# Another program order in the RWKV mixers: the merges of a head pair move behind the projections of the next pair

## The chip, the cores and the metric

The kernel runs on one core of a Trainium2 chip. The metric is the device time of one execution in microseconds. Three runs of the kernel before stand on record.

## The reference, cut to what matters

A first block of two layers (each a token mixer with RWKV and convolution branches, then a mixture of experts, "PEER") is followed by a second block with other mixers. The change lies in the RWKV branch of the two token mixers.

```python
def rwkv_scan(decay, k, v, kk, a, r, s0, reverse):
...
    def step(S, inp):
        w_t, k_t, v_t, kk_t, a_t = inp[:5]
        sa = jnp.einsum('bhvk,bhk->bhv', S, kk_t)
        S = (S * w_t[:, :, None, :]
             - sa[..., None] * (kk_t * a_t)[:, :, None, :]
             + v_t[..., None] * k_t[:, :, None, :])
        y = jnp.einsum('bhvk,bhk->bhv', S, inp[5]) if emit else None
        return S, y
...
def rwkv_branch(zr, p, s0, emit):
...
    for d, (w1d, a1d) in enumerate(((w1f, a1f), (w1b, a1b))):
        wlog = -jax.nn.softplus(-(p['w0'][d] + jnp.tanh(w1d) @ p['w2'][d])) - 0.5
        decay = jnp.exp(-jnp.exp(wlog.astype(jnp.float32)))
        a = jax.nn.sigmoid(a1d @ p['a2'][d] + p['a0'][d])
        kd = k * (1 + (a - 1) * p['k_a'])
        S, y = rwkv_scan(heads(decay), heads(kd), heads(v), kk, heads(a),
                         heads(r) if emit else None, s0[d], reverse=(d == 1))
```

There are 16 heads of 64 channels, a forward and a backward scan, and 512 tokens (256 of context, 256 of the sequence). Layer 0 needs the outputs of all tokens, layer 1 those of the sequence alone.

## The kernel before, in words

The scan is computed in chunks of 64 tokens. Two heads (a pair, j = 0 to 7) fill the 128 partitions. For each pair `rwkv_a` projects k, r and v (the tiles `zps`, 72 matmuls, each product in three parts of high and low halves, all issued by the helper at L264), norms k (`ssps`, L425), makes decay and gate (`wps` and `aps`, L442, each followed by a tanh on ScalarE, L445), and then the chunks' score matrices (`scps`, L491), transposes (`btps`, L505; `vps`, L515) and the bonus (`bops`, L524).

`rwkv_inv` inverts the triangular score matrices: `tri_inverse` in layer 0, `tri_inverse16` in layer 1. Each has two halves. The head takes blocks to DRAM and back, runs a forward substitution row by row on VectorE (`tm`, `xt`: 31 steps in layer 0, 15 in layer 1) and sends the result through DRAM into `xl`. The tail, here called the merges, joins the inverted blocks by 32x32 matmuls into `q` (L686 and L692 in layer 0: 128 of them; L750, L759, L772 and L780 in layer 1: 384 of them) with copies on ScalarE and VectorE between the groups.

`rwkv_b` is the serial chain over the 8 chunks in both directions: `bp`, a copy to `bs`, `up`, a copy to `uv`, `zp`, a scaling into `zb`, and the outputs `yp`; then mean and variance (`mps`, L619; `vaps`, L624). The loop runs chain j-1 after `rwkv_a(j)` and the inversion of pair j.

Independent work fills the gaps: convolution tiles (C), gate projections (G, the tiles `gtps`, 24 matmuls each), modulation weights (A, `adaps`), the gate of the RWKV output (I, also `zps`), layer norm sums (M, V), the convolution's output product (B, `yb`). The table `PLAN` says at which named places (`pop("a")`, `pop("z")`, `pop("i")`, `pop("c0")` and so on) one of each kind is issued. A scheduler turns the program into one queue per engine: the program order sets the priority, and a ready instruction may pass one that is not ready. Psum tiles come from shared pools of two buffers each: "mm" for all projections and fills, "rk" for `ssps` through `q`.

Of the kernel before, what the change touches and what calls it, by code (L numbers as in the profile page):

```python
# [27 lines left out]
NPAIR = 8  # L28
# [4 lines left out]
PLAN = (({'s1': 'C', 'a': 'GGAA', 'i': 'AC'}, {'c4': 'GGA', 'c5': 'A', 'c7': 'AC'}, {'z': 'GAMIGI', 'i': 'V', 'c0': 'S', 'c1': 'S'}, {'c0': 'OA', 'c1': 'O', 'c2': 'O', 'c3': 'B', 'c4': 'A'}),  # L33
        ({'z': 'G', 's0': 'AC', 's1': 'GCAAG', 'i': 'G'}, {'z': 'G', 'c0': 'G', 'c1': 'AA', 'c2': 'C'}, {'z': 'I', 'i': 'I', 'c0': 'MVS', 'c7': 'S'}, {}))
BUMP = (200, 400)
W16 = (0, 1, 1)
# [142 lines left out]
class Core:  # L179
# [225 lines left out]

    def rwkv_a(self, l, j, emitc):

        nc, rp, pr = self.nc, self.rp, self.prk
        Tr = T2 if emitc else TX
        emit = lambda c: emitc or c < 4  # L410
# [22 lines left out]
        SC, KR, BT, UV, kds = [], [], [], [], []  # L433
        pcs = rp.tile([P, 2, 8], F32, tag="pcs", name="pcs", bufs=2)
# [3 lines left out]
        for q, (src, bias, res, name) in enumerate(((self.tw, self.w0h, lds, "ld"), (self.za, self.a0h, ths, "th"))):  # L438
# [4 lines left out]
            for d in range(2):  # L443
                t = tl(name)
                nc.scalar.activation(t, pss[d], AF.Tanh, scale=0.5, bias=bias[:, d, j:j + 1])  # L445
                res.append(t)
        self.pop("z")
        for d in range(2):
            ld, th = lds[d], ths[d]

# [68 lines left out]
        bo = tl("bo", "bo", 2)  # L519
# [4 lines left out]
        nc.tensor.matmul(ps[:, :Tr], self.blk, bo[:, :Tr], start=True, stop=True)  # L524
        nc.vector.tensor_mul(bo[:, :Tr], v[:, :Tr], ps[:, :Tr])
        nc.scalar.activation(bo[:, :Tr], bo[:, :Tr], AF.Identity, bias=self.par(l, "lnx_b", j))
        return SC, KR, BT, UV, pcs, bo

    def rwkv_inv(self, l, ops):
        (self.tri_inverse, self.tri_inverse16)[W16[l]]([[t[:, 0].rearrange("p c h t -> p (c h) t") for t in q]  # L530
                                                        for q in ops[0]], self.prk, ("rk", "rk"))

    def rwkv_b(self, l, j, emitc, o, ops):

# [101 lines left out]
    def tri_inverse(self, SC, pp, tag):  # L636


        nc, rp = self.nc, self.rp
        ND = len(SC)  # L640
        NL = 32 * ND
        s0 = self.dp.tile([2, 2, 16, 32, 32], F32, tag="inv0", name="inv0")
        s1 = self.dp.tile([2, 2, 16, 16, 2, 32], F32, tag="inv1", name="inv1")
        xd = rp.tile([64, 16, 32], F32, tag="i2", name="xd", bufs=4)
        halves = [(t, slice(8 * n, 8 * n + 8)) for n, t in enumerate(SC[0])]
        for b in range(2):
            bs = slice(32 * b, 32 * b + 32)
            for n, (t, us) in enumerate(halves):
                nc.vector.transpose(xd[bs, us], t[bs, :, bs])
                if ND > 1:  # L650
                    nc.sync.dma_start(s0[1, b, us].rearrange("u s t -> s u t"), SC[1][n][bs, :, bs])
            nc.sync.dma_start(s0[0, b].rearrange("u s t -> s u t"), xd[bs])

        am = rp.tile([2 * NL, 32, 32], F32, tag="am", name="am", bufs=1)
        xt = rp.tile([2 * NL, 16, 32], F32, tag="xt", name="xt", bufs=1)
        nc.gpsimd.memset(xt, 0.0)
        for h in range(2):
            hs = slice(h * NL, h * NL + NL)
            nc.sync.dma_start(am[hs], s0[:ND].rearrange("d b u s t -> (d b u) s t"))
            nc.gpsimd.memset(xt[hs].rearrange("p a b -> p (a b)")[:, h::34], 1.0)  # L660
        nc.gpsimd.memset(am.rearrange("p a b -> p (a b)")[:, ::33], 1.0)
        tm = rp.tile([2 * NL, 16 * 32], F32, tag="i2", name="tm", bufs=4)
        for t in range(1, 32):
            n = (t + 1) // 2
            q = tm[:, :n * (t + 1)].rearrange("p (a b) -> p a b", b=t + 1)
            nc.vector.tensor_mul(q, xt[:, 0:n, 0:t + 1], am[:, t, 0:t + 1].unsqueeze(1).to_broadcast([2 * NL, n, t + 1]))
            nc.vector.tensor_reduce(xt[:, 0:n, t], q, axis=AX.X, op=ALU.add)
        for h in range(2):
            nc.sync.dma_start(s1[:ND, :, :, :, h].rearrange("d b u s t -> (d b u) s t"), xt[h * NL:h * NL + NL])
        xl = [rp.tile([64, 16, 32], F32, tag="i2", name=f"xl{d}", bufs=4) for d in range(ND)]  # L670
        for d in range(ND):
            for b in range(2):
                nc.sync.dma_start(xl[d][32 * b:32 * b + 32], s1[d, b].rearrange("u s h t -> (s h) u t"))

        lo, hi = slice(0, 32), slice(32, 64)
        nat = rp.tile([64, 16, 32], F32, tag="i2", name="nat", bufs=4)
        nc.vector.transpose(nat, xl[0])
        for d, (a, b) in enumerate(((lo, hi), (hi, lo))[:ND]):
            if d == 1:
                for q in (lo, hi):  # L680
                    for n, (_, us) in enumerate(halves):
                        nc.vector.transpose(SC[1][n][q, :, q], xl[1][q, us])
            n_ = nat if d == 0 else xl[1]
            q1 = pp.tile([P, 16, 32], F32, tag=tag[d], name="q1")
            for u in range(16):
                nc.tensor.matmul(q1[b, u, :], SC[d][u // 8][a, u % 8, b], n_[a, u, :], start=True, stop=True)  # L686
            qs = rp.tile([64, 16, 32], F32, tag="i2", name="qs", bufs=4)
            nc.scalar.copy(qs[b], q1[b])
            q2 = pp.tile([P, 16, 32], F32, tag=tag[d], name="q2")
            for u in range(16):  # L690
                tr = xl[0][b, u, :] if d == 0 else SC[1][u // 8][b, u % 8, b]
                nc.tensor.matmul(q2[a, u, :], qs[b, u, :], tr, start=True, stop=True)  # L692
            for n, (_, us) in enumerate(halves):
                nc.scalar.copy(SC[d][n][a, :, b], q2[a, us])
        for q in (lo, hi):
            for t, us in halves:
                nc.scalar.copy(t[q, :, q], xl[0][q, us])

    def tri_inverse16(self, SC, pp, tag):
# [26 lines left out]
        for t in range(1, 16):  # L726
            q = tm[:, :t * t].rearrange("p (a b) -> p a b", b=t)
# [6 lines left out]
        for d in range(ND):  # L734
            nc.gpsimd.memset(xl[d], 0.0)
            for b in range(2):
                for q in range(2):
                    r = slice(32 * b + 16 * q, 32 * b + 16 * q + 16)
                    nc.sync.dma_start(xl[d][r, :, 16 * q:16 * q + 16], s1[q, d, b].rearrange("u s t -> s u t"))
        lo, hi = slice(0, 32), slice(32, 64)  # L740
        copy = (nc.scalar.copy, nc.vector.tensor_copy)
        nt, q1, qs = [], [], []
# [220 lines left out]
    def mixer(self, l, xin, xout):  # L963
        nc, tc = self.nc, self.tc
        emitc = l == 0
        T = T2 if emitc else TX
        gs = self.dp.tile([16, P, T2], F32, tag="gs", name="gs", bufs=1)
        with ExitStack() as mx:
# [16 lines left out]
            with ExitStack() as rx:  # L985
                self.rp = rx.enter_context(tc.tile_pool(name="rp", bufs=2, reuse_waits="tile"))
                self.fp = rx.enter_context(tc.tile_pool(name="fp", bufs=1, reuse_waits="tile"))
                self.prk = rx.enter_context(tc.tile_pool(name="prk", bufs=2, reuse_waits="tile", space=PSUM))
                self.pch = rx.enter_context(tc.tile_pool(name="pch", bufs=2, reuse_waits="tile", space=PSUM))
                self.og = og  # L990
                self.rwkv_setup(l, emitc)
                self.fill_setup(l)
                nxt = None
                units = self.tail_units(l, T, craw, gs, o, og, yd)
                units["C"] = [partial(self.conv_tile, l, j, T, craw) for j in range(NPAIR)]
                units["G"] = [partial(self.gate_tile, l, m, T, gs) for m in range(16)]
                units["A"] = self.ada_units(l)
                self.units = units
                for j in range(NPAIR + 1):
                    self.at = PLAN[l][0 if j == 0 else max(1, j - NPAIR + 3)]  # L1000
                    self.bump = BUMP[l] if j >= NPAIR - 1 else 0
                    ops = nxt
                    if j < NPAIR:
                        nxt = self.rwkv_a(l, j, emitc)
                        self.pop("a")
                        self.rwkv_inv(l, nxt)
                        self.pop("i")
                    if ops:
                        self.rwkv_b(l, j - 1, emitc, o, ops)
                self.at = {"z": "".join(q * len(units[q]) for q in "CGIMVS") + "BOB" * 4 + "B" * 8 + "A" * 24}  # L1010
                self.bump = 0
                self.pop("z")
# [492 lines left out]
    def gdn(self, wp, proj, sel, cm, R, dst):  # L1505
# [4 lines left out]
        for j in range(6):  # L1510
            w = lambda tap: self.par2("dn_conv", tap * 6 + j)
            c, s = cv[:, j], qkv[:, j]
# [16 lines left out]
        q, k, v = cv[:, 0:2], cv[:, 2:4], cv[:, 4:6]  # L1529
# [45 lines left out]
        SC = wp.tile([P, 16, P], F32, name="gsc")  # L1575
        dv = dm.rearrange("p c h t -> p (c h) t")
        for c in range(4):
            for p in range(2):
# [4 lines left out]
                nc.vector.tensor_mul(SC[0:64, u:u + 2, 64:128], ps[0:64, 0:2, 64:128], dv[:, u:u + 2])  # L1583
                nc.vector.tensor_mul(dv[:, u:u + 2], dv[:, u:u + 2], cm[:, 1].unsqueeze(1).to_broadcast([64, 2, 64]))
                nc.vector.tensor_mul(SC[0:64, u:u + 2, 0:64], ps[0:64, 0:2, 0:64], dv[:, u:u + 2])
        (self.tri_inverse, self.tri_inverse16)[W16[2]]([[SC[:, 0:8], SC[:, 8:16]]], self.prk, ("rk",))
        o = wp.tile([P, 2, TX], F32, name="go", tag="go")
        S = None
        for c in range(4):
# [237 lines left out]
```

## Time and profile before

| | us |
|---|---|
| median of three runs | 5080.45 (5070.31 to 5085.05) |
| the profiled execution, own time | 5079.12 |
| its span in the trace | 5077.3 |
| TensorE (PE) busy | 4865.7 (96%) |
| VectorE (DVE) busy | 3378.1 (67%) |
| ScalarE (ACT) busy | 2388.9 (47%) |

About 1.8 us of the execution lie outside the span. The mean granted clock of TensorE is 0.972 of full speed. The pair loop of layer 0 runs from about 51 to 970 us, that of layer 1 from about 2771 to 3540 us; the rest of the time belongs to stages whose code is the same before and after. Matmuls are pipelined: the distance from one start to the next says what one costs, the printed duration of one row is longer.

### The profile page before, as it was taken

To read this page: it belongs to the slowest core of one execution; us is meant where nothing else is said; L and a number is where in the kernel's file an instruction comes from. 1 tells how busy PE (TensorE), PEld (TensorE's weight loads), DVE (VectorE), ACT (ScalarE), POOL (GpSimd) and SP (SyncE) were. 2 spreads that over 40 slices of the span, in tenths; PEclk is the share of its full clock that TensorE was granted. 3 is DMA by queue.
4 is the path that set the end of the run, shared out by engine and by line. 5 is a ranking of instruction groups with operands and counts; after the bars stand their busy time and mean duration, and the time that the engine had idled before them with its cause. 6 is when DMAs were issued, how large, how long until landed. Compare 5 with 4: busy or idle time off the path is not lost.

```text
span 5077.3 us, 81799 instructions
## 1 busy us (share of the span) xinstructions
PE 4865.7 (96%) x31202; PEld 4044.7 (80%) x31202; DVE 3378.1 (67%) x7538; ACT 2388.9 (47%) x4390; POOL 245.8 (5%) x629
## 2 busy tenths in 40 slices
PE   8899998999999999999999999999899999988989
PEld 6677776678888888888887787877889888877887
DVE  5788878558997455555555565756798666654754
ACT  4345444433765322222223445555467545565564
POOL 0111111100000000000000011111000000000000
PEclk9999999999999999999999899998999999998999
DMA  4333333542445644444442332323656877633444
GB/s 141 108 95 89 92 84 96 183 146 100 187 171 208 202 138 149 141 148 139 145 145 70 107 90 73 98 69 93 214 204 225 301 241 243 225 102 111 155 156 152
DMA packets 437132, 740.73 MB, mean 146 GB/s; under 512 B 132675, under 2 KB 276739, under 8 KB 433027
## 3 DMA queue, kind: packets, MB, share of 16 engines
q1 hardware_dynamic: 435218, 732.81, 44.9%
q8 instruction: 245, 4.01, 0.3%
q10 hardware_dynamic: 1520, 2.69, 0.2%
q14 instruction: 149, 1.21, 0.1%
HBM read 622.89 MB, written 112.49 MB: 145 GB/s over the span
## 4 chain that ended last, share of the span: by engine, by line
PE 80%; DVE 10%; ACT 5%; DMA 4%; issue 1%; SPq 0%; POOL 0%; ACTq 0%; DVEq 0%; POOLq 0%
PE s L264 17%; PE v L1188 14%; PE acc L1200 6%; PE zps L264 5%; PE wps L1133 4%; PE adaps L285 3%; PE gtps L264 2%; PE ops L264 2%; PE qps L264 2%; PE acc L1421 2%; DVE wlo L246 2%; PE yp L566 1%; PE up L590 1%; PE zp L595 1%; PE y L264 1%
## 5 line engine op out<-in xcount | busy, mean ns | idle before, releaser
L264 PE MATMUL s<-h,whi 128*128 128x512 f32 (+1 forms) x4096 | 1034.2, 341 | 2.3 <-ACT whi L244 1.8
L246 DVE TENSOR_TENSOR wlo<-wraw,whi 128x1024 fp32r<-128x1024 f32 (+2 forms) x606 | 725.0, 1199 | 451.7 <-ACT whi L244 441.8
L244 ACT CAST whi<-wraw 128x1024 fp32r<-128x1024 f32 (+2 forms) x606 | 622.9, 1029 | 817.9 <-PE s L264 274.9
L264 PEld LDWEIGHTS s<-h,whi 128*128 128x128 f32 x4096 | 706.8, 191 | 78.7 <-ACT whi L244 3.0
L264 PE MATMUL s<-h,wlo 128*128 128x512 f32 (+1 forms) x2048 | 699.6, 342 | 11.7 <-DVE wlo L246 11.7
L960 ACT CAST vh<-vraw 128x1024 fp32r<-128x1024 f32 x256 | 264.6, 1051 | 648.9 <-PE v L1188 474.9
L264 PEld LDWEIGHTS s<-h,wlo 128*128 128x128 f32 x2048 | 390.6, 191 | 50.9 <-DVE wlo L246 13.8
L1188 PE MATMUL v<-ah,vl 128*128 128x512 f32 x1024 | 401.4, 392 | 0.0
L1188 PE MATMUL v<-al,vh 128*128 128x512 f32 x1024 | 400.3, 391 | 0.0
L1188 PE MATMUL v<-ah,vh 128*128 128x512 f32 x1024 | 393.1, 391 | 0.5
L961 DVE TENSOR_TENSOR vl<-vraw,vh 128x1024 fp32r<-128x1024 f32 x256 | 308.8, 1221 | 101.0 <-ACT vh L960 100.5
L1265 DVE SCALAR_TENSOR_TENSOR x<-v,mod,x 128x256 f32<-128x256 f32 x512 | 220.1, 478 | 204.9 <-PE v L1188 204.6
L264 PE MATMUL zps<-h,whi 128*128 128x512 f32 (+3 forms) x896 | 295.7, 408 | 18.5 <-DVE lz L371 7.5
L1133 PE MATMUL wps<-qt,pt 128*128 128x128 f32 x1536 | 229.7, 285 | 0.8 <-DVE pt L1131 0.6
L1188 PEld LDWEIGHTS v<-ah,vh 128*128 128x128 f32 x1024 | 190.9, 188 | 47.7 <-ACT ah L960 7.3
L1133 PEld LDWEIGHTS wps<-qt,pt 128*128 128x128 f32 x1536 | 201.7, 190 | 33.9 <-ACT pt L1129 21.0
L1188 PEld LDWEIGHTS v<-al,vh 128*128 128x128 f32 x1024 | 192.2, 188 | 45.3 <-DVE al L961 3.9
L1188 PEld LDWEIGHTS v<-ah,vl 128*128 128x128 f32 x1024 | 192.2, 188 | 40.5 <-issue 1.4
L264 PEld LDWEIGHTS zps<-h,whi 128*128 128x128 f32 (+1 forms) x896 | 169.8, 198 | 58.6 <-issue 19.9
L285 PE MATMUL adaps<-adaw,cs 128*2 128x128 f32 x1536 | 203.5, 272 | 6.6 <-DMA adaw<-ada 4.8
L264 PE MATMUL zps<-h,wlo 128*128 128x512 f32 (+3 forms) x448 | 178.9, 400 | 1.4 <-DVE wlo L246 1.3
L580 POOL COPY krp<-kr 64x128 f32<-64x128 f32 (+1 forms) x448 | 151.1, 337 | 546.2 <-PE yp L566 308.6
(636 smaller groups left out, 10061.8 us busy)
## 6 DMA issues: line engine op xcount, KB each, us to landing
wraw<-peu SPq DMA_DIRECT2D x256, 512.0 KB, 4.1
vraw<-pev SPq DMA_DIRECT2D x256, 512.0 KB, 4.5
wraw<-win SPq DMA_DIRECT2D x139, 512.0 KB, 3.6
adaw<-ada SPq DMA_DIRECT2D x96, 512.0 KB, 3.8
wd<-ws SPq DMA_DIRECT2D x24, 2048.0 KB, 6.8
wt<-wd SPq DMA_DIRECT2D x32, 1024.0 KB, 7.2
wraw<-w_q SPq DMA_DIRECT2D x32, 512.0 KB, 3.6
gd<-ge SPq DMA_DIRECT2D x64, 256.0 KB, 2.4
```

Source lines behind the costliest of these rows:

```text
L244: nc.scalar.copy(hi, raw)
L246: nc.vector.tensor_sub(lo, raw, hi.bitcast(F32))
L264: nc.tensor.matmul(out, w[wi][:, k, :], a[ai][:, k, ts], start=n == 0, stop=n == 3 * ko - 1)
L285: nc.tensor.matmul(ps[0:2, i * P:i * P + P], self.cs[:, k, :], w[:, k, :], start=k == 0, stop=k == KO - 1)
L580: nc.gpsimd.tensor_copy(krp[hs, 0:n, hh], KR[d][hs, 0:n, c * 64:c * 64 + 64])
L960: self.nc.scalar.copy(hi, src)
L961: self.nc.vector.tensor_sub(lo, src, hi.bitcast(F32))
L1133: nc.tensor.matmul(ps[:, t, :], pt, qt[:, t1 + t], start=True, stop=True)
L1188: nc.tensor.matmul(ps[:, m, :], va[i][wi][:, ms], aa[i][ai], start=n == 0, stop=n == 3 * GI - 1)
L1200: nc.tensor.matmul(acc[b][c], aa[i][ai][:, bs], va[i][wi][:, c * 512:c * 512 + 512], start=g + i + n == 0, stop=g == P // GI - 1 and i == ...
L1265: nc.vector.scalar_tensor_tensor(x[:, k, ts], src[:, m, ts], self.mod[l][:, 40 + k, s:s + 1], x[:, k, ts], op0=ALU.mult, op1=ALU.add)
L1421: nc.tensor.matmul(acc[b][c], u[ai][:, f, b * P:b * P + P], w[wi][:, c * 512:c * 512 + 512], start=f + n == 0, stop=f == 31 and n == 2)
```

## The change

The loop over pairs starts one turn earlier, and each turn has a new order. `rwkv_a` becomes a generator in two halves: a1 through the tanh of `wps` and `aps`, a2 the rest. The inversions become generators too: the head up to the loads of `xl`, the tail with the merges. Turn j issues a2(j), the head of inversion j, the chain of pair j-1, a1(j+1), and then the merges of pair j. Before, the merges of pair j stood directly behind their head and ahead of chain j-1, and a1(j+1) behind that chain. The fills of place "z" stood inside `rwkv_a` and now stand behind the inversion's head; the extra turn (j = -1) pops "z" as well, with the first row of `PLAN`. `PLAN` and `BUMP` keep their values.

```diff
-        self.pop("z")
+        yield
         for d in range(2):
             ld, th = lds[d], ths[d]
...
-        return SC, KR, BT, UV, pcs, bo
+        yield SC, KR, BT, UV, pcs, bo
...
                 nc.sync.dma_start(xl[d][32 * b:32 * b + 32], s1[d, b].rearrange("u s h t -> (s h) u t"))
+        yield
...
-                nxt = None
+                nxt = ops = None
...
-                for j in range(NPAIR + 1):
-                    self.at = PLAN[l][0 if j == 0 else max(1, j - NPAIR + 3)]
+                for j in range(-1, NPAIR + 1):
+
+                    self.at = PLAN[l][0 if j < 1 else max(1, j - NPAIR + 3)]
                     self.bump = BUMP[l] if j >= NPAIR - 1 else 0
-                    ops = nxt
-                    if j < NPAIR:
-                        nxt = self.rwkv_a(l, j, emitc)
+                    ops, inv = nxt, iter(())
+                    if 0 <= j < NPAIR:
+                        nxt = next(make)
                         self.pop("a")
-                        self.rwkv_inv(l, nxt)
-                        self.pop("i")
-                    if ops:
+                        inv = self.rwkv_inv(l, nxt)
+                        next(inv)
+                    self.pop("z")
+                    self.pop("i" if 0 <= j < NPAIR else "")
+                    if j > 0:
                         self.rwkv_b(l, j - 1, emitc, o, ops)
+                    if j + 1 < NPAIR:
+                        make = self.rwkv_a(l, j + 1, emitc)
+                        next(make)
+                    for _ in inv:
+                        pass
```

What the scheduler makes of it is read from the queues of the two programs. The rows give line, operation, output and inputs, shape, and how often it repeats; lines of the changed kernel are one to three higher.

The first place is TensorE's queue in layer 1 at the merges of a middle pair, in the kernel before: the end of the merges, with projections of the next pair (`zps`) between the groups and behind them.

```order
L772 MATMUL q_25725<-nat,sc 32x32 x16
L264 MATMUL zps<-h_23068,whi 128x512
L264 MATMUL zps<-h_23067,wlo 128x512
L772 MATMUL q_25744<-xl_25564,sc 32x32 x16
L780 MATMUL q_25763<-xl_25563,qs_25742 32x32 x16
L780 MATMUL q_25782<-sc,qs_25761 32x32 x16
L264 MATMUL zps<-h_23067,whi 128x512
L264 MATMUL zps<-h_23068,whi 128x512
L264 MATMUL zps<-h_23067,wlo 128x512
L619 MATMUL mps<-oT,blk 128x256
```

The same place in the changed kernel.

```order
L775 MATMUL q_26312<-nat,sc 32x32 x16
L264 MATMUL gtps<-h_23067,whi 128x256
L264 MATMUL gtps<-h_23068,whi 128x256
L264 MATMUL gtps<-h_23067,wlo 128x256
L285 MATMUL adaps<-adaw,cs 2x128
L775 MATMUL q_26331<-xl_25564,sc 32x32 x16
L783 MATMUL q_26350<-xl_25563,qs_26329 32x32 x16
L285 MATMUL adaps<-adaw,cs 2x128 x2
L783 MATMUL q_26369<-sc,qs_26348 32x32 x16
L492 MATMUL scps<-kr,be 128x2x64 x4
L582 MATMUL bp<-uv,sc 128x128
L492 MATMUL scps<-kr,be 128x2x64 x4
```

The projections of the next pair, with `mps` and `vaps`, now stand ahead of the merges; behind the merges follow the score matrices of the next pair and the first step of this pair's chain.

The second place is TensorE's queue at the start of layer 1, in the kernel before, behind the projections of the first pair.

```order
L264 MATMUL zps<-h_23067,wlo 128x512
L425 MATMUL ssps<-sq,blk 128x512
L442 MATMUL wps<-tw,w_23239 128x512
L264 MATMUL gtps<-h_23067,whi 128x256
L264 MATMUL gtps<-h_23068,whi 128x256
L264 MATMUL gtps<-h_23067,wlo 128x256
```

The changed kernel there.

```order
L264 MATMUL zps<-h_23067,wlo 128x512
L426 MATMUL ssps<-sq,blk 128x512
L443 MATMUL wps<-tw,w_23274 128x512
L285 MATMUL adaps<-adaw,cs 2x128 x3
L443 MATMUL wps<-tw,w_23274 128x512
L443 MATMUL aps<-za,w_23274 128x512
L285 MATMUL adaps<-adaw,cs 2x128 x10
L443 MATMUL aps<-za,w_23274 128x512
```

One G (24 rows of `gtps`) has left this place; it now stands behind the first 48 `zps` of the layer, ahead of the 72 of the first pair.

The third place is TensorE's queue in layer 0 at the end of the merges of pair 6, in the kernel before.

```order
L264 MATMUL zps<-h_121,wlo 128x512
L692 MATMUL q_6721<-sc,qs 32x32 x16
L264 MATMUL zps<-h_121,whi 128x512
L264 MATMUL zps<-h_122,whi 128x512
L264 MATMUL zps<-h_121,wlo 128x512
```

The changed kernel there.

```order
L285 MATMUL adaps<-adaw,cs 2x128 x2
L694 MATMUL q_7389<-sc,qs 32x32 x16
L831 MATMUL lnm<-csum,onesd 128x512
L492 MATMUL scps<-kr,be 128x2x64 x8
L591 MATMUL up<-bs_1723,sc 128x128
L582 MATMUL bp<-uv,sc 128x128
L289 MATMUL adaps<-ident,adarow 128x2 x2
```

The rest of the projections of pair 7 stood behind these merges and now stands ahead of them; the score matrices of pair 7 follow at once.

## Rows read from the trace of the kernel before

**Rows 1.** The page: busy time of the engines, and the chain that ended last.

```profile
PE 4865.7 (96%) x31202; PEld 4044.7 (80%) x31202; DVE 3378.1 (67%) x7538; ACT 2388.9 (47%) x4390; POOL 245.8 (5%) x629
PE 80%; DVE 10%; ACT 5%; DMA 4%; issue 1%; SPq 0%; POOL 0%; ACTq 0%; DVEq 0%; POOLq 0%
```

**Rows 2.** Stretches of layer 0: start:end length, busy per engine, PE clock, DMA.

```profile
300.00:800.00 500.00, 492.17 (x3365) 366.40 (x3364) 401.25 (x1018) 246.39 (x530) 63.43 (x184) 1.00 0.34 92
850.00:900.00 50.00, 36.85 (x219) 28.34 (x220) 42.32 (x115) 25.88 (x68) 23.07 (x35) 0.90 0.37 103
```

**Rows 3.** Stretches of layer 1, in the same columns.

```profile
3000.00:3400.00 400.00, 386.12 (x3992) 319.87 (x3993) 264.00 (x723) 213.38 (x489) 63.13 (x181) 0.95 0.32 86
2974.00:2990.00 16.00, 16.00 (x151) 13.52 (x150) 4.62 (x12) 6.07 (x12) 0.59 (x1) 0.58 0.00 1
3485.00:3498.00 13.00, 11.86 (x283) 10.93 (x276) 7.46 (x18) 10.17 (x21) 0.00 (x0) 0.53 0.05 15
3498.00:3503.00 5.00, 5.00 (x20) 4.55 (x19) 2.01 (x7) 1.03 (x4) 0.00 (x0) 0.51 0.18 58
```

**Rows 4.** PE's timeline in layer 0, chain and `adaps` in turn: start, duration, work.

```profile
427.69 0.39 PE L566 MATMUL yp<-sc,uv 128*128 128x128 f32 x2
427.92 0.39 PE L590 MATMUL up<-bs,sc 128*128 128x128 f32 x2
428.23 0.38 PE L285 MATMUL adaps<-adaw,cs 128*2 128x128 f32 x2
428.54 0.49 PE L595 MATMUL zp<-uv,bt 128*128 128x128 f32 x2
```

**Rows 5.** PE's timeline, end of layer 0: merges 6, transposes 7, first merge of 7.

```profile
798.49 0.72 PE L264 MATMUL zps<-h,whi 128*128 128x512 f32 x2
838.15 0.60 PE L505 MATMUL btps<-ident,be 128*128 128x128 f32 x4
902.39 1.19 PE L686 MATMUL q<-nat,sc 32*32 32x32 f32 x32
```

**Rows 6.** PE's timeline in layer 1, start of the layer, with waits in brackets.

```profile
2788.73 0.70 PE L264 MATMUL zps<-h,whi 128*128 128x512 f32 x2 [3.78 <-DVE lz L371]
2810.78 0.28 PE L264 MATMUL gtps<-h,wlo 128*128 128x256 f32 x1
2810.90 0.40 PE L264 MATMUL gtps<-h,whi 128*128 128x256 f32 x2
2817.91 0.28 PE L289 MATMUL adaps<-ident,adarow 2*128 2x2 f32 x2 [1.30 <-ACT adarow L287]
2819.95 1.84 PE L491 MATMUL scps<-kr,be 64*128 64x128 f32 x16 [1.76 <-DVE be L477]
```

**Rows 7.** PE's timeline in layer 1, end of a middle pair's merges and behind them.

```profile
2980.03 1.73 PE L780 MATMUL q<-sc,qs 32*32 32x32 f32 x29
2984.41 1.05 PE L264 MATMUL zps<-h,whi 128*128 128x512 f32 x2
2988.39 0.62 PE L264 MATMUL zps<-h,whi 128*128 128x512 f32 x2
```

**Rows 8.** PE's timeline, end of layer 1: merges 6, score matrices 7, merges 7.

```profile
3409.74 1.73 PE L780 MATMUL q<-sc,qs 32*32 32x32 f32 x29
3433.94 1.16 PE L491 MATMUL scps<-kr,be 64*128 64x128 f32 x16
3450.41 0.64 PE L595 MATMUL zp<-uv,bt 128*128 128x128 f32 x2
3481.81 1.20 PE L750 MATMUL q<-nt,sc 32*32 32x32 f32 x64
3485.90 1.93 PE L759 MATMUL q<-xl,qs 32*32 32x32 f32 x63 [0.51 <-ACT qs L753]
3491.38 1.72 PE L772 MATMUL q<-nat,sc 32*32 32x32 f32 x29 [0.63 <-DVE nat L763]
```

**Rows 9.** ACT's groups in layer 1, 2750 to 3600 us: one of the table loads.

```profile
L445 ACT ACT_TABLE_LOAD x8 | 10.3, 1283 | 0.1
```

More of the change, by code (lines that the diff above doesn't have):

```diff
@@ L526, in rwkv_a @@
         nc.scalar.activation(bo[:, :Tr], bo[:, :Tr], AF.Identity, bias=self.par(l, "lnx_b", j))
-        return SC, KR, BT, UV, pcs, bo
+        yield SC, KR, BT, UV, pcs, bo
     def rwkv_inv(self, l, ops):
-        (self.tri_inverse, self.tri_inverse16)[W16[l]]([[t[:, 0].rearrange("p c h t -> p (c h) t") for t in q]
-                                                        for q in ops[0]], self.prk, ("rk", "rk"))
+        return (self.tri_inverse, self.tri_inverse16)[W16[l]]([[t[:, 0].rearrange("p c h t -> p (c h) t") for t in q]
+                                                               for q in ops[0]], self.prk, ("rk", "rk"))
     def rwkv_b(self, l, j, emitc, o, ops):
@@ L739, in tri_inverse16 @@
                     nc.sync.dma_start(xl[d][r, :, 16 * q:16 * q + 16], s1[q, d, b].rearrange("u s t -> s u t"))
+        yield
         lo, hi = slice(0, 32), slice(32, 64)
@@ L1585, in gdn @@
                 nc.vector.tensor_mul(SC[0:64, u:u + 2, 0:64], ps[0:64, 0:2, 0:64], dv[:, u:u + 2])
-        (self.tri_inverse, self.tri_inverse16)[W16[2]]([[SC[:, 0:8], SC[:, 8:16]]], self.prk, ("rk",))
+        for _ in (self.tri_inverse, self.tri_inverse16)[W16[2]]([[SC[:, 0:8], SC[:, 8:16]]], self.prk, ("rk",)):
+            pass
         o = wp.tile([P, 2, TX], F32, name="go", tag="go")
```

## The prediction

> **What bounds the kernel now.** I read the page first. TensorE is busy for 96% of the span and is 80% of the chain that ended last; VectorE stands at 67% and ScalarE at 47% [rows 1]. A change that only reorders work, as this one does, can therefore win or lose only what TensorE loses: idle time, time at half clock, and the extra distance at a change from one kind of matmul to another.
>
> So I went through both pair loops in stretches. In layer 0 the middle pairs are full: 492.17 us busy of 500, clock 1.00 [rows 2]. Nothing is left there for an order to win. The end of layer 0 is different: 850 to 900 us has TensorE busy for 36.85 of 50, clock 0.90 [rows 2]. That is chain 6 running nearly bare while VectorE does the substitution of pair 7, and it holds 13.15 us of idle time.
>
> Layer 1 loses more in its middle: 386.12 of 400 us busy, clock 0.95 [rows 3]. A clock of 0.95 as a mix of its two levels (1.2 and 2.4 GHz) means a tenth of the stretch at half speed, some 40 us. The last merges of two pairs start at 2980.03 [rows 7] and 3409.74 [rows 8], five pairs apart, so a pair takes 85.9 us and the stretch holds 4.66 pairs: 8.6 us of half clock and 3.0 us of idle time for each. The timeline says where. At a pair's merges TensorE is busy for 16.00 of 16 us, and the clock is 0.58 [rows 3], so 13.4 us at half. The `zps` pairs that follow inside the dip print 1.05 us each where they print 0.62 us later [rows 7].
>
> **The change, part by part.** No matmul is removed, apart from regrouping. What moves:
>
> *Layer 0, middle pairs.* The order of TensorE hardly differs. In a middle pair I count 132 runs of one kind against 126. A change of kind costs little: two `yp` start 0.23 us ahead of the next pair, the two `up` behind them take 0.31 us until `adaps` starts [rows 4], so 0.09 us. Six changes a pair are 0.5 us, and over six pairs 3 us. Below that stands nothing, as many changes are free (`yp` to `up` here). I take half: **+1.5 us** (0 to +3).
>
> *Layer 0, end.* The last merge of pair 6 ends near 798.5 us, the transposes of pair 7 near 838.5, and merges 7 begin at 902.4 [rows 5]. The last 64 us of this are the substitution's latency, which the change leaves alone. The 40 us ahead of it hold the scores and transposes of pair 7 and the rest of its projections. Of that rest, by the order, 33 `zps`, the norm, `wps`, `aps`, gates and some `adaps`, in all 19.5 us at the distances they have in the trace, now lie ahead of merges 6. Scores and transposes alone are bounded by layer 1, where they take 16.5 us from 3433.94 to 3450.41 [rows 8]. So 40 - 19.5 - 16.5 = 4 us of this stretch disappear, a gain of 4. Against it stand about 26 `adaps` (3 us) and 33 `yb` (4.7 us) that filled chain 6 and now come behind merges 7: 7.7 us, if nothing there is idle to take them. I take the sum of both, **+3.5 us** (-4 to +8).
>
> *Layer 1, start.* One G moves from behind `wps` to the place ahead of the 72 projections. A `gtps` costs 0.12 us [rows 6], 24 of them 2.9 us. Where they stood, TensorE now runs out of work sooner: it already waits 1.30 us for `adarow` and 1.76 us for `be` there [rows 6]. Where they go there is a wait of 3.78 us for `lz` [rows 6], but `gtps` draws on the same two "mm" buffers whose release is that wait, so they stand in it too and don't fill it. **+3 us** (0 to +3).
>
> *Layer 1, middle.* Runs of fill between the merges and the chain's steps go from 39 to 47 a pair. Each extra run is two changes, 0.18 us; 8 of them on six pairs are 8.6 us, and half of it, **+4 us** (0 to +8.6), is taken as above. The merges stand barer. Where they are bare today, at the end of the layer, they wait 0.51 us for `qs` and 0.63 us for `nat` [rows 8] for each pair; eight `gtps` (1 us) remain between the groups and cover part. Half, 0.57 us on seven pairs, is **+4 us** (0 to +8).
>
> *Layer 1, clock.* The dip stays, because the merges that it comes with stay. It shrinks if the full-size `zps` no longer stand in it; it grows because `scps` and chain steps follow now in place of dense projections. The bare merges of pair 7 have 0.53 over 13 us and 0.51 over 5 us [rows 3], 17.1 us at half, where the average pair has 8.6. Half of the difference of 8.5 us is lost: 4.3 us a pair, +30 us on seven pairs. If the whole dip went, half of 8.6 us on seven pairs, 30 us, would come back. With these ends on either side I take **0** (-30 to +30).
>
> The Trainium skill, "TensorE: Matmul & The Clock Gate", section "HAM oscillation — how this bites in real kernels", has the clock fall because TensorE idles between groups of matmuls. By that rule merges that are packed together would be harmless and the clock term could only fall, so the sum would be what it is or less. The row of 16.00 busy us at clock 0.58 differs from it [rows 3]: here the clock fell without idle time, among 32x32 matmuls, so the upper end is kept.
>
> *Layer 1, end.* From the end of merges 6, 3411.5, to merges 7, 3481.8, are 70.3 us [rows 8]. Scores and transposes (16.5 us) and then chain and substitution to 3481.8 (31.4 us) need 48. Of the 22.3 us between, 12.2 us of projections and gates move ahead, the rest is waits and half clock: a gain of 10 if merges 6, now bare, cost nothing. If they stand as bare as merges 7, which take about 16 us from 3481.81 [rows 8] and are at half clock from 3485 on [rows 3], they lose some 6. **-4 us** (-10 to +6).
>
> *ScalarE.* The regrouped tanh and exponentials need ten activation table loads less, 1283 ns each [rows 9], 12.8 us. ScalarE is busy for 47% [rows 1], and TensorE's work hides this, so 0.
>
> The sum: 1.5 + 3.5 + 3 + 4 + 4 + 0 - 4 = **+12 us**. On the profiled execution's 5079.1 us, which already contains the 1.8 us around the span, this gives 5091. The median of the runs is 1.3 us above that execution, and the runs spread over 15 us, so I leave it: about **5090 us**.
>
> **The rivals.** A measurement of this kernel tells a change of about 0.3%, 15 us, from none.
>
> *Slower, by the clock in layer 1.* If `scps` and the chain's first steps keep the clock down as long as in the bare merges of pair 7, the +30 us apply and the time is 5120. It passes the 0.3% once the dips grow by 1 us a pair (3.5 us in all on top of 12). For it: 0.50 to 0.53 wherever merges stand bare [rows 3]. Against it: scores and chain are partly filled with `adaps`, and less dense work stands in the dip to pay for it.
>
> *Faster, by the same dips.* If the dense rows leave the dip and the clock recovers as fast, up to 30 us come back: 5060. For it: the `zps` at 1.05 us [rows 7]. Against it: whatever stands behind the merges pays instead.
>
> *Faster, by the ends.* If chain 6, which starts at once behind merges 6, is filled in both layers, the idle 13 us [rows 2] and the 10 us at the end of layer 1 go, without the 7.7 us and the 6 us: some 5068 with the other terms. Against it: VectorE runs at 42.32 of 50 us there [rows 2], and the substitution keeps its length.
>
> *No effect.* The scheduler lets ready instructions pass others, and the queues of layer 0 stay nearly alike. If the small terms are all free, 5076 to 5080.
>
> **How the numbers follow.** Forecast, a few us slower within 0.3%: 0.36. Clock slower, or several small terms at their upper ends (4 + 4 us more, 5 at the end of layer 0, 10 at that of layer 1): 0.33. No effect: 0.11. The two faster ones together: 0.20, half of it ending above 5060. Range 5055 to 5125: it leaves out the clock's upper end with all small terms on top, and the two gains together. Faster 0.20, same 0.47, slower 0.33. The forecast's own range is 5075 to 5096.
>
> **What would show it.** Layer 0's middle still at 98% busy and its pairs within 0.6 us of before; 24 `gtps` gone from behind the first `wps` of layer 1 and the wait for `be` longer by up to 3 us; the clock of layer 1's middle within 0.93 to 0.97, and its pair period within 2 us of 85.9; merges 7 closer to merges 6 in both layers, by about 24 and 22 us. I would be wrong if a pair of layer 1 took 80 us or 92 us, since seven pairs multiply whatever the merges' new place does to the clock, or if VectorE's substitution waited behind the new a1 work and the chain had to wait for it.

## The result and the profile after

The changed kernel takes 5132.5 us (5129.22 to 5134.62, 4 runs) where the kernel before takes 5082.75 us (5070.31 to 5087.95, 4 runs): a ratio of 1.0107 with a 95% interval of 1.0091 to 1.0124, 50 us slower. The forecast was 5090 us in a range of 5055 to 5125, so the time lies above the range. The profiled execution has a span of 5132.4 us, 55 more than that of before.

The page's busy times and the chain that ended last, of the changed kernel:

```profile
PE 4924.7 (96%) x31202; PEld 4087.8 (80%) x31202; DVE 3384.1 (66%) x7538; ACT 2376.7 (46%) x4380; POOL 251.3 (5%) x629
PE 83%; DVE 8%; ACT 4%; DMA 3%; issue 1%; POOL 0%; SPq 0%; ACTq 0%; DVEq 0%; POOLq 0%
```

TensorE does the same 31202 matmuls and is busy 59 us longer than in [rows 1]. So the time did not go into waits; the same matmuls took longer. The mean granted clock over the whole span is 0.959 to 0.961 in the four runs of the changed kernel; in the listed runs of the kernel before, it is 0.970 to 0.975. Stretches of the changed kernel (start:end, length, busy per engine, granted clock, DMA):

```profile
300.00:800.00 500.00, 488.82 (x3345) 366.43 (x3345) 396.15 (x1007) 244.75 (x528) 63.57 (x185) 0.99 0.33 91
850.00:900.00 50.00, 41.68 (x216) 33.19 (x214) 37.49 (x112) 20.48 (x57) 17.68 (x32) 0.86 0.36 94
3000.00:3400.00 400.00, 389.75 (x3893) 314.56 (x3894) 237.37 (x626) 181.54 (x427) 58.84 (x150) 0.83 0.27 73
3192.00:3224.00 32.00, 30.59 (x346) 24.22 (x341) 17.16 (x35) 7.94 (x18) 0.12 (x1) 0.52 0.08 26
3224.00:3284.00 60.00, 59.28 (x406) 48.63 (x404) 37.44 (x113) 32.49 (x79) 14.41 (x35) 1.00 0.39 104
```

The middle of layer 1 went from a clock of 0.95 [rows 3] to 0.83, with a little less idle time than before (10.25 us of 400, where [rows 3] leave 13.88). One pair, the last two rows, shows it: 32 us nearly all at half clock, then 60 us at full clock. In the kernel before, the dip of the pair shown was 13.4 us of 16 [rows 3]. The timeline of the changed kernel inside this dip:

```profile
3206.05 1.91 PE L783 MATMUL q<-sc,qs 32*32 32x32 f32 x32
3207.89 2.07 PE L492 MATMUL scps<-kr,be 64*128 64x128 f32 x8
...
3218.17 4.85 PE L285 MATMUL adaps<-adaw,cs 128*2 128x128 f32 x22
3223.47 0.29 PE L289 MATMUL adaps<-ident,adarow 2*128 2x2 f32 x2 [0.45 <-ACT adarow L287]
3223.69 1.17 PE L492 MATMUL scps<-kr,be 64*128 64x128 f32 x16
3224.79 1.25 PE L285 MATMUL adaps<-adaw,cs 128*2 128x128 f32 x10
```

The merges end at 3207.9, and for 15 us more everything behind them is slow: 8 `scps` in 2.07 us, and 22 `adaps` in 4.85 us. At 3223.7 the clock is back: 16 `scps` in 1.17 us, 10 `adaps` in 1.25 us. In the kernel before, projections of the next pair followed the merges, and the clock was back within 7 us of their end [rows 7].

The pairs of layer 1 follow each other at 95.0 us in place of 85.9: the last merges of two pairs, three apart, in the changed kernel:

```profile
3110.28 1.91 PE L783 MATMUL q<-sc,qs 32*32 32x32 f32 x32
...
3395.28 1.91 PE L783 MATMUL q<-sc,qs 32*32 32x32 f32 x32
```

To weigh clock against waits I added up the granted clock and the busy time of TensorE in stretches of 1 us from the last `nps` (the norm's sums of squares, which open a mixer) of layer 1's mixer to the first one behind it. Time at half clock is twice what the clock lacks to 1; half of it is lost. Loop is the length of that stretch. The kernels of the experiments, whose times follow below, stand in the same table. Each row is one profiled execution. How far two executions differ is seen where layer 1 has the same order: 150.2 and 136.6 us in the old one, 273.1 and 252.5 in the new one. A difference of half-clock time of some 20 us can therefore be chance.

| kernel | loop us | at half clock us | idle us |
|---|---|---|---|
| before | 832.2 | 150.2 | 55.4 |
| changed | 887.7 | 273.1 | 48.4 |
| new order in layer 0 alone | 828.5 | 136.6 | 56.6 |
| new order in layer 1 alone | 879.8 | 252.5 | 48.9 |
| merges ahead of a1 | 865.9 | 180.8 | 69.9 |
| convolution behind | 879.1 | 225.2 | 57.5 |
| extra dense work | 903.9 | 225.4 | 56.3 |
| modulation first | 894.5 | 293.6 | 57.6 |
| wide merges, old order | 796.5 | 88.8 | 51.6 |
| wide merges, new order | 802.2 | 95.6 | 48.2 |
| merges cut in two, old order | 811.6 | 105.9 | 53.1 |
| the same, convolution ahead | 885.8 | 177.5 | 88.0 |

The changed kernel's loop is 55.5 us longer. Half of 122.9 us more at half clock is 61.4, and 7.0 us less idle time gives 54.4: the account closes within 1.1 us. For the other kernels with the same matmuls it misses by 2 to 12 us (most with the modulation first: 73.9 by the account, 62.3 measured), so it gives the size and not the last microseconds.

### The profile page after: what moved, and what is told of

Its sections match the earlier page's. It is cut to its first block, busy times and chain, and to the rows that moved or that the text cites. A ratio compares the mean times of both kernels' runs of the same rounds, so it can differ in the third digit from the quotient of the medians.

```text
span 5132.4 us, 81763 instructions
## 1 busy us (share of the span) xinstructions
PE 4924.7 (96%) x31202; PEld 4087.8 (80%) x31202; DVE 3384.1 (66%) x7538; ACT 2376.7 (46%) x4380; POOL 251.3 (5%) x629
## 4 chain that ended last, share of the span: by engine, by line
PE 83%; DVE 8%; ACT 4%; DMA 3%; issue 1%; POOL 0%; SPq 0%; ACTq 0%; DVEq 0%; POOLq 0%
PE s L264 18%; PE v L1199 14%; PE acc L1211 7%; PE zps L264 5%; PE wps L1144 4%; PE adaps L285 3%; PE gtps L264 3%; PE ops L264 2%; PE scps L492 2%; PE qps L264 2%; DVE wlo L246 2%; PE acc L1432 2%; PE zbps L264 2%; PE up L591 1%; PE zp L596 1%; PE yp L567 1%
## 5 line engine op out<-in xcount | busy, mean ns | idle before, releaser
L964 DVE TENSOR_TENSOR vl<-vraw,vh 128x1024 fp32r<-128x1024 f32 x256 | 308.6, 1222 | 102.5 <-ACT vh L963 101.7
L264 PE MATMUL zps<-h,whi 128*128 128x512 f32 (+3 forms) x896 | 279.8, 390 | 13.2 <-ACT h L352 6.3
L285 PE MATMUL adaps<-adaw,cs 128*2 128x128 f32 x1536 | 233.4, 294 | 4.8 <-DMA adaw<-ada 3.5
L1199 PEld LDWEIGHTS v<-ah,vh 128*128 128x128 f32 x1024 | 191.0, 188 | 47.6 <-ACT ah L963 7.3
L264 PEld LDWEIGHTS zps<-h,whi 128*128 128x128 f32 (+1 forms) x896 | 162.3, 189 | 48.2 <-ACT h L352 9.3
L285 PEld LDWEIGHTS adaps<-adaw,cs 128*2 128x2 f32 x1536 | 117.0, 89 | 82.5 <-issue 17.3
```

The lines of the kernel that those rows point to most:

```text
L264: nc.tensor.matmul(out, w[wi][:, k, :], a[ai][:, k, ts], start=n == 0, stop=n == 3 * ko - 1)
L285: nc.tensor.matmul(ps[0:2, i * P:i * P + P], self.cs[:, k, :], w[:, k, :], start=k == 0, stop=k == KO - 1)
L964: self.nc.vector.tensor_sub(lo, src, hi.bitcast(F32))
L1199: nc.tensor.matmul(ps[:, m, :], va[i][wi][:, ms], aa[i][ai], start=n == 0, stop=n == 3 * GI - 1)
```

## The experiments

The theory is that the place of the merges in TensorE's queue sets how long the clock stays at half speed. The rival is that the new order costs by itself, by waits, changes of kind of matmul and the place of the fills.

**The new order in one layer alone.** One loop of each kind stands behind a test of the layer (for the second kernel the test is `l == 0`).

```diff
-                for j in range(-1, NPAIR + 1):
+                if l == 1:
+                    for j in range(NPAIR + 1):
...
+                else:
+                    for j in range(-1, NPAIR + 1):
...
```

> The new order in layer 0 alone, the old one in layer 1. Clock theory (the loss is half-clock time around the merges of layer 1): the time is that of before plus what layer 0 costs by the trace of the changed kernel, 0 to 8 us: 5080 to 5091, ratio 1.000 to 1.002, and layer 1 has its 0.95 back between 3000 and 3400 us. Rival (the loss comes from more changes of kind of matmul and waits everywhere the order is new, both layers): half or more of the 50 us stay, 5105 or more.

> The new order in layer 1 alone. Clock theory: nearly the whole loss, 5125 to 5137, granted clock 0.82 to 0.86 in the middle of layer 1, pairs of about 95 us, some 30 us at half clock behind each pair's merges. Rival (changes of kind and waits in both layers): 25 us or less of the loss, 5108 or less.

Layer 0 alone: 5086.53 us, a ratio to before of 1.0014 (1.0002 to 1.0026), clock 0.96 between 3000 and 3400 us. Layer 1 alone: 5129.3 us, 1.0098 (1.0076 to 1.0120), clock 0.84 between 3000 and 3400 us. Both are what the clock theory gave. Nearly the whole loss is layer 1's.

**Merges ahead of the first half of the next pair.** The edit against the new order in layer 1 alone, cut to what moves:

```diff
...
-                        if j + 1 < NPAIR:
-                            make = self.rwkv_a(l, j + 1, emitc)
-                            next(make)
                         for _ in inv:
                             pass
+                        if j + 1 < NPAIR:
+                            make = self.rwkv_a(l, j + 1, emitc)
+                            next(make)
...
```

> As the new order in layer 1 alone, but the merges of pair j are issued ahead of the first half of pair j+1, so that dense projections of the next pair stand behind and between them again. Clock theory: the half-clock stretch goes back to 9 to 14 us a pair, the pair to 85 to 88 us, the time to 5075 to 5095. Rival (the loss comes from the split of the projections and the place of the fills z, which this kernel keeps): 5115 or more.

It takes 5115.91 us, 1.0075 (1.0052 to 1.0099): outside the range of the clock theory, just inside that of the rival. The table says why. Time at half clock falls from 252.5 to 180.8 us, worth 36 us, as the theory has it, but 21 us more of idle time eat most of that. The middle stretch of this kernel shows both:

```profile
3000.00:3400.00 400.00, 382.49 (x3773) 305.25 (x3770) 248.93 (x653) 205.36 (x453) 57.97 (x154) 0.91 0.30 80
```

So the clock responds to the place of the merges, but this place costs waits of its own; the run settles nothing alone.

**Which fill stands behind the merges.** In the middle pairs, once the convolution ahead of the modulation, once the modulation first. The entry of `PLAN` for these pairs, cut out of its line, in the one kernel and then in the other:

```diff
-{'z': 'G', 'c0': 'G', 'c1': 'AA', 'c2': 'C'}
+{'z': 'G', 'c0': 'G', 'c1': 'C', 'c2': 'AA'}
```

```diff
-{'z': 'G', 'c0': 'G', 'c1': 'AA', 'c2': 'C'}
+{'z': 'A', 'c0': 'A', 'c1': 'GG', 'c2': 'C'}
```

> As the new order in layer 1 alone, but in the middle pairs the convolution fill (128x256 projections on the full array) is popped ahead of the two modulation fills (two columns of the array), so that dense work stands among the score matrices behind the merges where the modulation stood. Same work, same order of pairs. Clock theory: the clock comes back earlier, 15 to 22 us at half a pair in place of 30, about 4 to 7 us a pair better: 5090 to 5112. Rival (order and waits of the merges themselves cost the time): the same as the new order in layer 1 alone, 5125 to 5137.

> The new order in layer 1 alone, with the fills of the middle pairs the other way round than in the convolution test: the modulation fills (two columns of the array) are popped first and so lie from the gate projections through the merges and the scores, the dense gate fills come in the chain. Same work. Clock theory: the clock falls no later and comes back no earlier, 28 to 40 us at half a pair: 5128 to 5165. Rival (what kind of fill stands there does not matter): the same as the order alone, 5122 to 5136, with the same half-clock time of about 250 us within 15.

With the convolution behind, 5130.4 us, 1.0104 (1.0078 to 1.0131): no better than the order alone, as the rival said. Half-clock time fell by 27 us, worth 14, and idle time rose by 9; the stretches at pairs 1 to 4 shrank to 17 to 21 us, those of the last three pairs, which have no full convolution fill behind them, did not (92 us together, 85 with the order alone), and that of pair 0, which has one, stayed at 27. Of the 14 us only some 5 would remain, and the time does not show them. With the modulation first, 5141.16 us, 1.0116 (1.0083 to 1.0150), and 293.6 us at half clock: in the range of the clock theory, outside the rival's. But the interval of this ratio overlaps that of the order alone, 1.0076 to 1.0120, and the half-clock time is 20 us above the changed kernel's: the direction fits the clock theory, and the size is not clear of the noise.

**Extra dense work behind the merges.**

```diff
+                        if 0 <= j < NPAIR:
+                            ps = self.prk.tile([P, 512], F32, tag="rk", name="warm")
+                            for n in range(14):
+                                nc.tensor.matmul(ps, self.h[0][:, n % KO, 0:P], self.h[0][:, n % KO, :],
+                                                 start=n == 0, stop=n == 13)
```

> The new order in layer 1 alone, with 14 extra full-array matmuls (128x512) behind the merges of each pair, whose result nobody reads: 3.2 us more work a pair at full clock. Clock theory: they end the half-clock stretch early (27 us a pair down to 20 or less) and so pay for themselves in part or wholly: 5115 to 5140, half-clock time in layer 1 below 200 us where the order alone had 252. Rival (the clock does not depend on what follows the merges; the loss is the order's): the extra work comes on top, 5150 to 5175, half-clock time 250 us or more.

It takes 5147.59 us, 1.0125 (1.0096 to 1.0155), between the two expectations, and so is its half-clock time, 225.4 us. Windows of this kernel around one pair's extra matmuls, which start at 3116.77:

```profile
3099.00:3121.00 22.00, 22.00 (x401) 20.16 (x396) 14.33 (x30) 8.30 (x19) 0.23 (x2) 0.51 0.05 14
3121.00:3127.00 6.00, 6.00 (x48) 4.94 (x47) 2.68 (x7) 0.21 (x1) 0.00 (x0) 1.00 0.00 0
3127.00:3142.00 15.00, 15.00 (x75) 12.92 (x74) 5.18 (x15) 3.73 (x12) 0.91 (x4) 0.54 0.14 27
```

Behind the dense matmuls the clock is back, at 3121. Six microseconds later it is down again, while `scps`, `btps` and chain steps run without a pause. So at this pair the work behind the merges lowered the clock again by itself; it did not only prolong the dip. A long second dip of this kind stands at three of the eight pairs. Behind the extra matmuls of pair 3 the clock stays up:

```profile
3220.00:3235.00 15.00, 15.00 (x125) 11.67 (x124) 10.15 (x24) 2.44 (x8) 0.00 (x0) 1.00 0.30 69
```

The extra work is some 26 us (the 3.2 us of the expectation at each of eight pairs). Against it stand 27 us less at half clock, worth 14, and 7 us more idle time, so it did not pay.

**The narrow merges taken away.** In layer 1, each group of 32x32 matmuls becomes one wide matmul, in the old and in the new order. These kernels leave out the products of single blocks that the inversion needs. One of the four places:

```diff
-            for u in range(16):
-                for b in (lo, hi):
-                    nc.tensor.matmul(q1[d][b, u, :], SC[d][u // 8][b, u % 8, b], (nt, xl)[d][d][b, u, :],
-                                     start=True, stop=True)
+            if ND > 1:
+                nc.tensor.matmul(q1[d], SC[d][0][0:64, 0:2, :], (nt, xl)[d][d], start=True, stop=True)
...
```

> The old order, with each group of 32x32 matmuls of layer 1's merges replaced by one matmul of 64 rows, 128 columns and 512 wide on the same inputs, so that the output is not the reference's; copies and dependencies stay. Clock theory: no half-clock stretch at the merges, half-clock time in layer 1 down from 150 to 60 to 100 us, and some 8 us of merges less a pair: 4985 to 5040.

> The new order in layer 1 alone, with the same replacement in the merges. Clock theory (the narrow merges start the half-clock stretch, the narrow work behind them prolongs it): with the start gone the two orders come close, 0 to 15 us above the old order with the same merges. Rival (the new order costs by waits, changes of kind and the split projections): the 50 us stay between the two kernels.

The old order takes 5036.88 us, the new one 5048.74 us, on the same chip. The two orders differ by 12 us, where with the narrow merges they differ by 50 (5129.3 against 5078.85 in the first pair of experiments). The middle of layer 1, the old order's row, then the new order's:

```profile
2980.00:3380.00 400.00, 391.35 (x2479) 298.25 (x2480) 271.53 (x743) 226.57 (x512) 66.24 (x185) 0.98 0.31 87
```

```profile
2980.00:3380.00 400.00, 392.21 (x2493) 298.16 (x2491) 279.53 (x748) 214.78 (x506) 72.25 (x185) 0.99 0.30 87
```

With the same order, the same split projections and the same fills, the clock of the new order is 0.99 once the merges are wide. This pair of runs tells the theories apart: in the middle pairs the order costs by the narrow merges it leaves without dense work around them. Of the 47.6 us between the loops of the two orders (879.8 against 832.2 in the table) 5.7 remain.

At the last two pairs the dips stay, though, with wide merges too: 54.6 of the 95.6 us at half clock in the new order lie there, and 44.4 of 88.8 in the old. The dip at pair 6 in the new order:

```profile
3390.00:3424.00 34.00, 32.48 (x108) 21.03 (x106) 24.10 (x49) 12.61 (x27) 0.12 (x1) 0.50 0.05 8
```

Wide merges of 64 rows, `scps` and `bp` follow each other there with hardly a projection between. So merges of 32x32 are not the only work at which the clock falls.

**The merges cut in two, in the old order.** The other way round: in layer 1, `tri_inverse16` yields ahead of `nat`, and its last two groups are issued behind the three projections of the next pair. `rwkv_a` yields behind each projection.

```diff
         copy[d](xl[d][b:b + 16, :, 16:32], q2[b:b + 16, :, 16:32])
+        yield
         nat = i2("nat")
...
+                        for n in range(4):
+                            if n == 3:
+                                for _ in inv:
+                                    pass
+                            next(make)
```

> The old order in both layers, but in layer 1 the merges are cut in two: the first two groups of pair j where they were, the last two (128 narrow matmuls) behind the three projections of pair j+1, so that 15 to 26 full-size projections stand between the two halves. Same work. Clock theory: the narrow stretch is cut in two short ones with dense work between, half-clock time in layer 1 down from 150 to 60 to 115 us, 5045 to 5075. Rival (the number of narrow merges sets the half-clock time, whatever stands between; or the wait for the second half costs as much): 5075 to 5100, half-clock time 140 us or more.

> As the split merges in the old order, with the convolution fill of the middle pairs popped ahead of the two modulation fills, which puts 47 to 53 projections between and inside the halves of the merges and the convolution's dense work ahead of the scores. Clock theory: half-clock time no more than in the split alone, 5040 to 5075. Rival (the fills are worth more where they covered the waits of chain and scores): 5075 or more, with more idle time than the split alone.

The cut alone takes 5060.94 us (12 runs) against 5074.6 of before: 0.9972 (0.9962 to 0.9982). It is faster than both kernels. Half-clock time is 105.9 us, 44 less than before; half of that and 2 us of idle time make 24.5, and the loop is 20.6 us shorter; the medians differ by 13.7. One pair of this kernel:

```profile
3130.00:3136.00 6.00, 6.00 (x127) 5.57 (x127) 3.06 (x9) 4.03 (x10) 0.93 (x4) 1.00 0.03 5
3136.00:3142.00 6.00, 4.80 (x187) 4.49 (x182) 3.79 (x7) 4.70 (x12) 1.83 (x2) 1.00 0.01 3
3142.00:3148.00 6.00, 6.00 (x42) 4.74 (x41) 3.47 (x9) 4.73 (x7) 0.00 (x0) 1.00 0.31 90
3148.00:3154.00 6.00, 6.00 (x113) 5.53 (x110) 3.13 (x4) 3.45 (x6) 0.00 (x0) 0.74 0.37 112
```

The first half of the merges (to 3142) passes at full clock, the projections between run at full clock, and only the second half brings the clock down.

With the convolution ahead it takes 5126.06 us, 1.0104 (1.0089 to 1.0119), as the rival expectation said, and outside the range of the clock theory. The loop has 88.0 us of idle time. The first lines of TensorE's waits of this kernel, 2770 to 3640 us (total, times, longest):

```profile
PE up L594 <- ACT bs L592: 22.1, 21, 2.3
PE ya L264 <- ACT whi L244: 7.6, 1, 7.6
PE zbps L264 <- ACT whi L244: 7.3, 6, 1.5
```

The chain's `up` waits for the copy to `bs` 21 times. And half-clock time did not stay at the cut's 105.9 us, it rose to 177.5. That change of fills is what it shares with the convolution test above, which had not paid either. Why the half-clock time rose is not shown.

## Why the prediction was wrong

**The step that failed** is "Layer 1, clock": "With these ends on either side I take **0** (-30 to +30)". It measured +61 us in the changed kernel's loop (half of 273.1 less 150.2), twice the upper end, and 51 us in the new order in layer 1 alone. The prediction's own sign of being wrong, a pair of 92 us, came: the pair takes 95.0. The mechanism was named, as the rival "Slower, by the clock in layer 1", and given 0.33 together with other mishaps; its size was wrong. The bound came from the longest dip in the trace of before, the 17.1 us at the bare merges of pair 7. Behind those merges, though, full-size projections follow; the timeline of the kernel before goes on from there with

```profile
3497.93 0.80 PE L264 MATMUL yb<-h,whi 128*128 128x256 f32 x2
```

In the new order `scps` and `adaps` follow, and a dip lasts about 30 us; the fill with `adaps`, which the prediction held against a long dip, did not end it (22 of them in 4.85 us, at half clock). The nearest row was near in the merges and not in what stands behind them. The order of the changed queue showed those rows before the run, and the sum did not price them.

The Trainium skill's rule that was weighed there ("TensorE: Matmul & The Clock Gate", section "HAM oscillation — how this bites in real kernels": the clock falls because TensorE idles between groups) is not what lowered the clock here, as far as the profile's busy time shows. In the extra-dense kernel the clock fell with 6.00 of 6 and 15.00 of 15 us busy, and the new order has less idle time than the old.

**Layer 0** came out near its sum: +1.5 and +3.5 us were forecast. By the profiled spans from the first `ssps` to layer 0's next `nps` it is 5.2 us; the test of layer 0 alone gave 0.14% (0.02% to 0.26%), some 7 us. That is in part luck. These terms priced the clock at nothing, and it fell here too, from 0.90 [rows 2] to 0.86 between 850 and 900 us. Time at half clock in layer 0, between the `nps` on either side of its mixer, is 37.5 us before and 71.7 in the changed kernel; the ten kernels with the old order in this layer have 37.5 to 54.6, the two with the new one 71.7 and 81.9. Half of that is more than the whole loss, so something gained against it; what did is not shown.

The middle cost more than the 0.6 us a pair that was allowed. The first transposes of two pairs, four apart, in the kernel before and then in the changed one, are 102.6 and 103.9 us a pair apart (102.5 to 103.1 in the ten kernels, 103.9 in both of the two):

```profile
320.23 0.66 PE L505 MATMUL btps<-ident,be 128*128 128x128 f32 x4 [0.28 <-DVE sc L495]
...
730.64 0.55 PE L505 MATMUL btps<-ident,be 128*128 128x128 f32 x3 [0.28 <-DVE sc L495]
```

```profile
321.68 0.66 PE L506 MATMUL btps<-ident,be 128*128 128x128 f32 x4 [0.27 <-DVE sc L496]
...
737.29 0.66 PE L506 MATMUL btps<-ident,be 128*128 128x128 f32 x4 [0.27 <-DVE sc L496]
```

**The end of layer 0 and of layer 1.** Merges 7 did move closer to merges 6. The changed kernel's rows, first layer 0 (the row behind merges 6 and the first of merges 7), then layer 1 (the last of merges 6, the first of merges 7):

```profile
826.20 1.12 PE L831 MATMUL lnm<-csum,onesd 128*128 128x512 f32 x2
...
901.38 0.81 PE L688 MATMUL q<-nat,sc 32*32 32x32 f32 x20 [1.39 <-DVE nat L679]
...
3491.57 1.73 PE L783 MATMUL q<-sc,qs 32*32 32x32 f32 x29
...
3542.32 0.85 PE L753 MATMUL q<-nt,sc 32*32 32x32 f32 x42
```

From 103.9 us [rows 5] to 75.2 in layer 0, and from 72.1 [rows 8] to 50.8 in layer 1: 29 and 21 us, forecast 24 and 22. Whether the gain of 4 us at the end of layer 1 came cannot be read cleanly. From the last `ssps` to the next mixer stage the changed kernel needs 193.7 us and that of before 180.1, 13.6 more, but merges 6, which take 15.2 us from 3478.1 to 3493.3, lie inside this stretch in the changed kernel alone. The clock of this end has dips of 34 us (3476 to 3511) and 20 us (3547 to 3569). In the kernel before there are four, 7, 3, 14 and 17 us: 14 us less in all, worth 7, where the term allowed some 6 for merges 6. These 7 us are part of the 61 above.

**The start of layer 1** came out inside its range, 0 to +3 us: counted from the last `nps`, the first score matrices start at 55.1 us in place of 53.2. Rows of the changed kernel:

```profile
2826.29 0.28 PE L289 MATMUL adaps<-ident,adarow 2*128 2x2 f32 x2 [2.62 <-DVE kr L471]
2827.76 0.80 PE L264 MATMUL zbps<-h,whi 128*128 128x256 f32 x2 [1.19 <-ACT whi L244]
```

The waits there are 3.8 us, against 3.1 us in [rows 6], and the wait for `lz` is still 3.8 us, now under `gtps`: the moved gate projections did not fill it.

**Idle time and changes of kind in layer 1**, +4 and +4, were wrong in sign for the first: idle time fell by 7 us. What the changes of kind cost cannot be told apart from what the account leaves open, 1.1 us here and up to 12 in other kernels.

**The rest of the program**, which the change does not touch, took some 9 us less in the profiled execution of the changed kernel than in that of before. So the profiled spans differ by 55 us although the two mixers differ by about 64. The stages behind layer 1's mixer are the larger part of it: the same code there took 1468 to 1478 us in the twelve profiled executions, most of all in that of before, so this looks like chance and not like a gain of the change.

**What stays open.** That the narrow merges of the middle pairs lower the clock is shown by the two kernels without them; which of the kinds behind the merges (64-row `scps`, two-column `adaps`, chain steps) does how much is not. With wide merges the same `scps` and `adaps` ran at 0.99 in the middle pairs, at the last pairs and behind some of the extra dense matmuls similar work at 0.50 and 0.54. Why the same work holds the clock in one place and not in the other was not separated.

## What to carry to other kernels

On a kernel whose TensorE is 96% busy, look at the granted clock of each stretch, and when an order is changed, read from the new queue what stands directly behind a narrow stretch, not only what stands in it. Dense matmuls between narrow ones can pay: the cut of the merges in two, with projections between, gained 0.28% with the same work. They need not: dense work added behind the merges cost more than it gave, and a fill moved there left more idle time where it had covered waits.

## What the runs showed of the hardware

Unexpected was that the clock fell to half while TensorE had not a single idle stretch (16.00 of 16 us at 0.58 [rows 3], 15.00 of 15 at 0.54 in the extra-dense kernel), and that behind 5 us of dense matmuls it came back, at one pair, for only 6 us.
